# Order of the products of a half chunk: one PSUM bank after the other, or the two in turn

## The chip, the core and the metric

The kernel runs on one core of a Trainium2 chip. What counts is the device time of one execution in microseconds (us), the median of several runs.

## The reference, cut to what matters

Two transformer-like blocks and a mixture of experts on 256 tokens of 2048 features, all in float32: a layer with attention and a convolution, a layer with a spatial gate, a second block with attention and a state space branch, and last 16,384 experts as two dense products with sparse weights. Nearly all the work is in products of the activations with large weight matrices:

```
k, v, q, za, glu, zb = split(h @ ev_w_in)          # layer 0, 2048 x 5632
x = x + gate * (mix @ ev_w_out)                     # 2048 x 2048
p = h @ od_w_in ; x = x + gate * (mixed @ od_w_out) # layer 1, 2048 x 6144 and 2048 x 2048
... h @ w_in_2, w_attn_up_2, w_ssm_up_2, w_out_2    # second block
A = gelu(h @ peer_u.T) * weights ; x = x + gate * (A @ peer_v)   # experts, 2048 x 16384 twice
```

Between them stand norms with a scale and a shift, and each layer's scale, shift and gate come from a vector times a matrix of their own (the modulation).

## The kernel before, in words

**Chunks and halves.** Every large matrix is cut into chunks of 512 rows by 512 columns (1 MB), which come from memory in the order of one long plan. A chunk is worked off in two halves of 256 rows, that is two row tiles (`a` = 0, 1) of 128 rows. To keep float32 precision each half is split in two parts: ScalarE rounds it to `hi` (tile `whi`), VectorE makes `lo` = raw - `hi` (tile `wlo`). The activations are split the same way, `act.h` and `act.l` (tiles `hh` and `hl`, or `Ah`/`Al`, `mixh`/`mixl` and so on). A product is then three matmuls, hi with h, hi with l and lo with h, added up in PSUM.

**`gemm_part`** (L622) takes one half at a time and makes four tiles of 128 output features (`n` = 0 to 3) by 256 tokens. The weights are the stationary operand. The accumulator `ps` is 128 x 4 x 256 floats, that is two PSUM banks: `n` = 0 and 1 lie in the first, 2 and 3 in the second (or `ps` is a list of two tiles of one bank each, then named `last`). A half is 2 x 4 x 3 = 24 matmuls of 256 columns. There are 970 halves in all; 866 of them go through `gemm_part`.

**`gemm_tok_part`** (L646) makes keys, values, queries and the like, with tokens on the partitions: the activations are stationary, the weights stream through in 512 columns, and the two tiles of 128 tokens (`tt`) have a bank each (tiles `q`, `pv`, `kv`, `kvc`). A half is 2 x 2 x 3 = 12 matmuls of 512 columns. It serves the other 104 halves (52 chunks: group 4 to 6 of `ev`, 0 to 3 of `od`, 1 to 6 of `w2`, four chunks each); the first 8 of them do so for two activations, so there are 112 runs of 12 matmuls.

**The last half of an output projection** (`tiles` given, `j` = 1) has an order of its own, `n` outside and `a` inside, so that each pair of tiles can be read as soon as it is complete. There are four such halves.

**Who makes what, and when.** The program is written out in one thread of Python code; each engine runs its instructions in the order in which they were written. A clock (`Clock`, L256) estimates as the code runs when each engine will be done and when each tile will be there. After each half, `fill` (L552) asks `side` (L570) which other steps (evictions, norms, attention, the experts' weights) fit beside the products, by these estimates and in steps of 0.2 us; then the next halves are split, up to three ahead. A chunk of a modulation's matrix goes to VectorE as a multiply-add (tile `adaacc`), or, where the clock says that the products are more than `AGE` = 4 us past its arrival (`start`, L558), to TensorE (tile `adaps`). So the order in which side work stands on the engines depends on the estimated time of each product. The estimate lets a matmul start when its operands are there, and knows nothing of banks.

**The activations** of layer 1, the second block and the experts (`Normed`, L2105) are made in four groups of four row tiles by `h_group` (L851), each shortly before the first product needs it: VectorE `hu`, ScalarE `hh`, VectorE `hl`, row tile by row tile.

`forget` (L1528) makes eight forget gates: 48 matmuls of 256 columns in a row, with 8 columns of stationary weights, all into one place of one bank (tile `fp`).

Of the kernel before, what the change touches and what calls it, by code (L numbers as in the profile page):

```python
# [20 lines left out]
D = 2048  # L21
# [12 lines left out]
# ---------------------------------------------------------------- host layout  # L34
# [120 lines left out]
# ---------------------------------------------------------------- the plan of weight traffic  # L155
# [100 lines left out]
class Clock:  # L256
    """When each engine is expected to be through with what it has been given, and each part of a tile to be written and read."""
# [23 lines left out]
    def slot(self, tag, bufs, tile):  # L281
        """A new tile in one of the slots of a tag: written after the slot's last tile has been used."""
        slots = self.slots.setdefault(tag, [])
        if len(slots) == bufs:
            i = 0
            if tag in ("ms", "raw"):
                i = min(range(bufs), key=lambda i: self.used(slots[i]) if slots[i] in self.read else math.inf)
            self.parts[tile.tensor.name] = {(0, 1 << 20): [0.0, None, self.used(slots[i]), None]}
            del slots[i]
        slots.append(tile.tensor.name)  # L290
        return tile
# [4 lines left out]
    def free_at(self, tag, bufs, n):  # L296
        """When n of a tag's slots will have been read."""
        at = [0.0] * (bufs - len(self.slots.get(tag, [])))
        for name in self.slots.get(tag, []):
            if name in self.read:  # L300
                at.append(self.used(name))
        return sorted(at)[n - 1] if len(at) >= n else math.inf

    def columns(self, at, n):
        """The tensor engine's time for n columns: its clock is halved after a period in which it was mostly idle."""
# [39 lines left out]
class Timed:  # L345
    """The core's engines; each instruction is also entered in the clock."""
# [64 lines left out]
class Thread:  # L411
    """Work beside the weight stream. It yields the engine of its next step, with the number of PSUM slots that step takes
    (and when what it needs is there, if that isn't the last step's end); "w" when it waits for other threads."""
# [6 lines left out]
class K:  # L420
# [9 lines left out]
    # ---- storage  # L430
# [3 lines left out]
    def ms(self, name, shape=(128, 512), hold=False):  # L434
        """A PSUM bank, until something else than the tensor engine has read it, or, on hold, until its release."""
        t = self.psm.tile(list(shape), F32, name=name, tag="ms", bufs=4)
        return self.hold("ms", 4, t) if hold else self.clock.slot("ms", 4, t)
# [29 lines left out]
    # ---- weight stream  # L467
# [22 lines left out]
    def prep_hi(self, force):  # L490
        """The rounded part of the next half of a weight chunk."""
# [19 lines left out]
    def prep(self, force=True):  # L511
        """The rest of the next half chunk."""
# [11 lines left out]
    def ahead(self):  # L524
        """Keeps the split parts in front of the products: LOOK halves, and HILOOK more of their rounded parts."""
# [12 lines left out]
    # ---- side work  # L538
# [5 lines left out]
    def post(self, ps, gen, prio=0, eng="a"):  # L544
        """Work on products, once the tensor engine is through with what it has been given."""
# [6 lines left out]
    def fill(self, lead=LEAD):  # L552
        """After each half chunk of products: side work while these run, then the next parts of the weights."""
# [4 lines left out]
    def start(self, t):  # L558
        """When the next step of a thread could start."""
# [39 lines left out]
    def finish(self, *ts):  # L599
        """Runs these threads to their end, and others as far as they wait for them."""  # L600
# [14 lines left out]
    # ---- products  # L615
# [6 lines left out]
    def gemm_part(self, ps, name, g, kc, i, n_kc, act, kt0=0, tiles=None):  # L622
        """tiles: the work that follows on each of the four tiles of 128 features as soon as it is complete."""
        mm = self.nc.tensor.matmul
        for j in range(2):
            hi, lo = self.take(name, g, kc, j)
            each = tiles if j == 1 else None
            for n, a in [(n, a) for n in range(4) for a in range(2)] if each else [(n, a) for a in range(2) for n in range(4)]:
                kt = kt0 + 4 * i + 2 * j + a
                first, last = (kt == kt0), (kt == kt0 + 4 * n_kc - 1)  # L630
                s = slice(n * 128, n * 128 + 128)
                o = ps[n // 2][:, n % 2, :] if isinstance(ps, list) else ps[:, n, :]
                mm(o, hi[:, a, s], act.h(kt), start=first and n % 2 == 0, stop=False, skip_group_check=True)
                mm(o, hi[:, a, s], act.l(kt), start=False, stop=False, skip_group_check=True)
                mm(o, lo[:, a, s], act.h(kt), start=False, stop=last, skip_group_check=True)
                if each and a == 1 and n % 2 == 1:
                    each(n - 1)
                    each(n)
            if not each:
                self.fill(QUIET if tiles else LEAD)  # L640
# [5 lines left out]
    def gemm_tok_part(self, name, g, kc, i, n_kc, acts, outs):  # L646
        """outs[i]: two [128 tokens, 512] accumulators of activation i."""
        nc = self.nc
        for j in range(2):
            hi, lo = self.take(name, g, kc, j)  # L650
            for act, out in zip(acts, outs):
                if act is not acts[0]:
                    self.side(LEAD)
                for a in range(2):
                    kt = 4 * i + 2 * j + a
                    first, last = (kt == 0), (kt == 4 * n_kc - 1)
                    for tt in range(2):
                        s = slice(tt * 128, tt * 128 + 128)
                        nc.tensor.matmul(out[tt], act.h(kt)[:, s], hi[:, a, :], start=first, stop=False)
                        nc.tensor.matmul(out[tt], act.h(kt)[:, s], lo[:, a, :], start=False, stop=False)  # L660
                        nc.tensor.matmul(out[tt], act.l(kt)[:, s], hi[:, a, :], start=False, stop=last)
# [8 lines left out]
    # ---- modulation vectors  # L670
    def chunk(self, it, raw):
        """A chunk of a modulation's weights, worked off when it has come in: by the vector engine if that has the time."""
# [10 lines left out]
    def ada_s(self, it, raw):  # L683
        """Layer 0's shift and scale, 512 columns at a time, of x (row 0 of each 32) and of the context (row 16);
        each of the four row blocks of a chunk has its own 32 rows."""
# [32 lines left out]
    def ada(self, it, raw, me=None):  # L718
        """Its share of the vector: products on the tensor engine, or sums kept for each of the partitions."""
# [60 lines left out]
    # ---- norms  # L780
    def rsqrt_steps(self, out, ss, n, shape, v=None):
        """out = 1/sqrt(ss/n + EPS), or 1/sqrt(v) of a given v."""
# [15 lines left out]
    def stat(self, ps, r, first, last):  # L798
        """ps[t, half] += the sum of r over its partitions, for 256 tokens in two halves."""
# [3 lines left out]
    def spread(self, name, r):  # L803
        """A value per token, [128, 2], as a row on every partition."""
# [19 lines left out]
    def gap(self, until):  # L824
        """Modulation products while the tensor engine would wait."""
# [8 lines left out]
    def now(self, gen):  # L834
        """Runs a generator to its end and returns its value."""
# [6 lines left out]
    def sumsq(self, xg, g, ps, n=4):  # L842
        """Adds group g's squares into ps."""
# [7 lines left out]
    def h_group(self, act, g, xg, r, scale, shift, name):  # L851
        """One group of features of the split of (x r) scale + shift."""
# [25 lines left out]
    # ---- start  # L878
# [74 lines left out]
    def wait_mod(self, *keys):  # L953
        """Works off the plan and the threads until these vectors are there."""
# [8 lines left out]
    # ---- attention pieces  # L963
    def headnorm(self, ps, nh, gains, rope, dests, name):
        """ps: two [128 t, >= nh*128] views; per head rms over features, gain (and rope), then
        transposed into dests (one [128 hd, 256] view per head)."""
# [45 lines left out]
    def rope_tables(self):  # L1012
        """Gained rope tables of q and k: [128 t, 2, 128] each."""
# [14 lines left out]
    # ---- layer 0  # L1028
    def layer0(self):
# [30 lines left out]
        # the first groups, as the modulation of their inputs comes in  # L1060
# [12 lines left out]
        # keys and values  # L1073
# [73 lines left out]
    def gated(self, g, ps, gate):  # L1147
        """x += gate * ps for one group of features."""
# [6 lines left out]
    def out_proj(self, name, act, gate, kcs=range(4), nstat=1):  # L1155
        """x += gate * (act @ w), and the sums of squares of the new x."""
# [59 lines left out]
    def sum_ch(self, tiles, square):  # L1216
        """Sum over the channels of two [128, 4, 256] tiles: on every partition, or of the squares, a column per half."""
# [97 lines left out]
    # ---- layer 1  # L1315
# [102 lines left out]
    # ---- second block  # L1418
    def block2(self):
        nc = self.nc  # L1420
        # the norm of x2 = (x r1) fg: with r1 = rsqrt(ss0 / D + EPS), its rsqrt times r1 is rsqrt(ss1 / D + EPS (ss0 / D + EPS))
# [12 lines left out]
        # u, forget gates, q, k, v  # L1434
# [93 lines left out]
    def forget(self, h, bfc):  # L1528
        """Cumulated log forget gates, laid out for the two-row bias products."""
# [101 lines left out]
    # ---- state space branch  # L1631
    def exact_exp(self, x, n, tmp):
        """x <- exp(x) by range reduction and a polynomial; tmp: three [128, n] views."""
# [13 lines left out]
        # 2^k in two halves, so that each stays a normal number  # L1647
# [10 lines left out]
    def reduce_angle(self, x, k):  # L1658
        """x <- x - 2 pi round(x / 2 pi), within the sine's range."""
# [7 lines left out]
    def sincos(self, s, c, x):  # L1667
        """s, c <- sin x, cos x of a reduced angle."""
# [7 lines left out]
    def ssm_params(self):  # L1676
# [13 lines left out]
        # per state: decay and angle  # L1690
# [10 lines left out]
        # per channel and state: the input matrix  # L1701
# [127 lines left out]
    # ---- experts  # L1829
    def peer(self):  # L1830
# [43 lines left out]
        def before(g):  # L1874
            """x with what the earlier passes have come to."""
# [61 lines left out]
    def topk(self, g, q, ready, sk, sel, prev):  # L1937
# [20 lines left out]
        # sums of pairs (a, b) of the two sorted lists; with (a + 1)(b + 1) > 16 a pair is never among  # L1958
        # the first 16, so b < 8 is enough for a > 0: position 16 + 8 (a - 1) + b
# [44 lines left out]
    def top16(self, val, idx, s, w):  # L2004
        """The 16 largest of each row of s in order, with their places; w is for working on."""
# [19 lines left out]
    def expert_weights(self, tk, sel):  # L2025
        """The dense weights of all experts and tokens, by products of one-hots, into DRAM."""
# [49 lines left out]
    # ---- all  # L2076
# [28 lines left out]
class Normed(Split):  # L2105
    """(x r) scale + shift; a group of features is made shortly before a product first needs it."""
# [12 lines left out]
class LazySplit(Split):  # L2119
    """The experts' activations; a group is finished when a product first needs it."""  # L2120
# [28 lines left out]
```

## Time and profile before

| | |
|---|---|
| median of 3 runs | 3248.22 us |
| lowest and highest run | 3244.9 and 3250.54 us |
| span of the profiled execution, first to last instruction | 3244.0 us |
| TensorE busy | 3181.7 us (98%), 24,560 matmul records |
| VectorE busy | 2180.6 us (67%) |
| ScalarE busy | 1448.3 us (45%) |

The profiled execution has no time of its own beside its span; the span lies 4.2 us below the median of the runs, and what lies around it is taken to be that much. In the trace a matmul's start is recorded and its end is modelled (its duration covers the way through the array, so that neighbours overlap): the pace of a stream is read from starts, not from durations. A float32 matmul that isn't split shows as two records. All instructions have the line of one helper (L393), so they are told apart by tiles. The names show the operands as output<-inputs.

### The profile page before, as it was taken

How to read it: one execution, taken by the hardware profiler on the slowest of the kernel's cores; microseconds unless marked ns; L12 is line 12 of the kernel's file. 1: busy time of each engine (PE TensorE's matmuls, PEld its weight loads, DVE VectorE, ACT ScalarE, POOL GpSimd, SP SyncE). 2: the span in 40 equal slices, each digit the busy share in tenths (PEclk: the TensorE clock that was granted, in tenths of full speed). 3: DMA queues.
4: the chain of work that ended last, by engine and by line, in shares of the span. 5: the costliest groups of instructions: out<-in, count | busy, mean ns of one | idle time of the engine just before them, and what ended most of it. 6: DMA issues, size and time to landing. Idle time of an engine off the chain costs nothing.

```text
span 3244.0 us, 58103 instructions
## 1 busy us (share of the span) xinstructions
PE 3181.7 (98%) x24560; PEld 2954.1 (91%) x24560; DVE 2180.6 (67%) x3266; ACT 1448.3 (45%) x1879; POOL 12.2 (0%) x24
## 2 busy tenths in 40 slices
PE   5999999999999999999999999999999999999999
PEld 3677789789997778999999999999999999999999
DVE  3488868877788877667789996555455445445544
ACT  2334544444445556444444554444344334434433
POOL 0000000000000000000000000000000000000000
PEclk8999999999999999999999999999999999999999
DMA  7878586788785655677755667665555555555653
GB/s 305 319 285 299 195 312 236 279 319 306 279 305 208 222 195 193 253 258 293 288 180 199 236 228 273 234 208 202 182 202 207 185 190 205 198 184 203 228 195 130
DMA packets 140484, 764.04 MB, mean 236 GB/s; under 512 B 12528, under 2 KB 45296, under 8 KB 53568
## 3 DMA queue, kind: packets, MB, share of 16 engines
q1 hardware_dynamic: 137248, 750.04, 64.1%
q0 software_dynamic: 1824, 6.37, 0.6%
q8 instruction: 192, 3.15, 0.4%
q10 hardware_dynamic: 1152, 3.93, 0.3%
q14 instruction: 68, 0.56, 0.0%
HBM read 739.32 MB, written 20.97 MB: 234 GB/s over the span
## 4 chain that ended last, share of the span: by engine, by line
PE 93%; DVE 3%; DMA 2%; ACT 1%; issue 0%; DVEq 0%; SPq 0%; ACTq 0%; POOLq 0%
PE ps L393 73%; PE q L393 5%; PE last L393 3%; PE adaps L393 3%; PE pv L393 2%; PE pw L393 2%; DMA raw<-in_ev_dram 1%; DVE wlo L393 1%; PE S L393 1%; PE kvc L393 1%; PE kv L393 1%; DMA raw<-in_evo_dram 1%; PE po L393 0%; PE bu L393 0%; DVE cacc L393 0%; PE py L393 0%
## 5 line engine op out<-in xcount | busy, mean ns | idle before, releaser
L393 DVE TENSOR_TENSOR wlo<-raw,whi 128x1024 fp32r<-128x1024 f32 x970 | 1181.9, 1222 | 847.9 <-PE ps L393 619.8
L393 ACT ACTIVATE whi<-raw 128x1024 fp32r<-128x1024 f32 x970 | 1023.0, 1059 | 1384.4 <-PE ps L393 1032.2
L393 PE MATMUL ps<-hh,whi 128*128 128x256 f32 x3904 | 1120.0, 287 | 16.2 <-ACT hh L393 12.1
L393 PE MATMUL ps<-hl,whi 128*128 128x256 f32 x3904 | 1109.2, 284 | 1.2
L393 PE MATMUL ps<-hh,wlo 128*128 128x256 f32 x3904 | 1108.0, 284 | 0.0
L393 PEld LDWEIGHTS ps<-hh,whi 128*128 128x128 f32 x3904 | 752.1, 193 | 56.9 <-issue 33.6
L393 PEld LDWEIGHTS ps<-hl,whi 128*128 128x128 f32 x3904 | 752.6, 193 | 3.9 <-DVE hl L393 3.6
L393 PEld LDWEIGHTS ps<-hh,wlo 128*128 128x128 f32 x3904 | 752.3, 193 | 0.0
L393 PE MATMUL ps<-Ah,whi 128*128 128x256 f32 x1920 | 543.5, 283 | 0.0
L393 PE MATMUL ps<-Al,whi 128*128 128x256 f32 x1920 | 543.4, 283 | 0.0
L393 PE MATMUL ps<-Ah,wlo 128*128 128x256 f32 x1920 | 543.4, 283 | 0.0
L393 PEld LDWEIGHTS ps<-Ah,whi 128*128 128x128 f32 x1920 | 368.6, 192 | 0.8 <-issue 0.8
L393 PEld LDWEIGHTS ps<-Al,whi 128*128 128x128 f32 x1920 | 368.6, 192 | 0.0
L393 PEld LDWEIGHTS ps<-Ah,wlo 128*128 128x128 f32 x1920 | 368.6, 192 | 0.0
L393 DVE SCALAR_TENSOR_TENSOR adaacc<-raw,silc,adaacc 128x1024 f32<-128x1024 f32 x126 | 158.2, 1279 | 9.4 <-DMA raw<-in_ada_dram 9.0
L393 PE MATMUL ps<-mixh,whi 128*128 128x256 f32 x416 | 119.0, 286 | 0.0
L393 PE MATMUL ps<-mixh,wlo 128*128 128x256 f32 x416 | 117.7, 283 | 0.7 <-DVE wlo L393 0.7
L393 PE MATMUL ps<-mixl,whi 128*128 128x256 f32 x416 | 117.6, 283 | 0.0
L393 PE MATMUL q<-whi,hh 128*128 128x512 f32 x256 | 102.9, 402 | 0.0
L393 PE MATMUL q<-whi,hl 128*128 128x512 f32 x256 | 99.9, 390 | 0.0
L393 PE MATMUL q<-wlo,hh 128*128 128x512 f32 x256 | 99.9, 390 | 0.0
L393 DVE SCALAR_TENSOR_TENSOR cacc<-ypad,pk,cacc 128x256 f32<-128x256 f32 x240 | 99.3, 479 | 0.0
(389 smaller groups left out, 3618.4 us busy)
## 6 DMA issues: line engine op xcount, KB each, us to landing
raw<-in_ada_dram SPq DMA_DIRECT2D x160, 1024.0 KB, 5.4
raw<-in_pu_dram SPq DMA_DIRECT2D x128, 1024.0 KB, 4.8
raw<-in_pv_dram SPq DMA_DIRECT2D x128, 1024.0 KB, 4.8
raw<-in_w_dram SPq DMA_DIRECT2D x60, 1024.0 KB, 4.8
raw<-in_od_dram SPq DMA_DIRECT2D x48, 1024.0 KB, 5.9
raw<-in_ev_dram SPq DMA_DIRECT2D x44, 1024.0 KB, 6.5
raw<-in_ada0s_dram SPq DMA_DIRECT2D x32, 1024.0 KB, 7.8
raw<-in_evo_dram SPq DMA_DIRECT2D x16, 1024.0 KB, 5.9
```

Source lines behind the costliest of these rows:

```text
L393: r = f(*args, **kw)
```

## The change

The three matmuls of a product no longer follow each other. In `gemm_part`, for each row tile `a`, the four tiles of features all take hi with h, then all take hi with l, then all take lo with h, and the tiles come in the order 0, 2, 1, 3, so that each matmul writes another bank than the one before it; before it were six in a row to one bank and then six to the other. The last half of an output projection keeps its order. In `gemm_tok_part` the two tiles of tokens, a bank each, come in turn; before it were three in a row to each. The numbers of matmuls, weight loads, bytes and every other instruction's own work are the same; the `start` flag still stands on the first matmul into a bank and on no other.

```diff
-            for n, a in [(n, a) for n in range(4) for a in range(2)] if each else [(n, a) for a in range(2) for n in range(4)]:
+            first, last = kt0, kt0 + 4 * n_kc - 1
+
+            def product(n, a, p):
                 kt = kt0 + 4 * i + 2 * j + a
-                first, last = (kt == kt0), (kt == kt0 + 4 * n_kc - 1)
-                s = slice(n * 128, n * 128 + 128)
                 o = ps[n // 2][:, n % 2, :] if isinstance(ps, list) else ps[:, n, :]
-                mm(o, hi[:, a, s], act.h(kt), start=first and n % 2 == 0, stop=False, skip_group_check=True)
-                mm(o, hi[:, a, s], act.l(kt), start=False, stop=False, skip_group_check=True)
-                mm(o, lo[:, a, s], act.h(kt), start=False, stop=last, skip_group_check=True)
-                if each and a == 1 and n % 2 == 1:
-                    each(n - 1)
-                    each(n)
-            if not each:
-                self.fill(QUIET if tiles else LEAD)
+                w = (hi, hi, lo)[p][:, a, n * 128:n * 128 + 128]
+                mm(o, w, act.l(kt) if p == 1 else act.h(kt), start=kt == first and n % 2 == 0 and p == 0, stop=kt == last and p == 2,
+                   skip_group_check=True)
+
+            if each:
+                for n in range(4):
+                    for a in range(2):
+                        for p in range(3):
+                            product(n, a, p)
+                    if n % 2 == 1:
+                        each(n - 1)
+                        each(n)
+                continue
+
+            for a in range(2):
+                for p in range(3):
+                    for n in (0, 2, 1, 3):
+                        product(n, a, p)
+            self.fill(QUIET if tiles else LEAD)
...
-                    for tt in range(2):
-                        s = slice(tt * 128, tt * 128 + 128)
-                        nc.tensor.matmul(out[tt], act.h(kt)[:, s], hi[:, a, :], start=first, stop=False)
-                        nc.tensor.matmul(out[tt], act.h(kt)[:, s], lo[:, a, :], start=False, stop=False)
-                        nc.tensor.matmul(out[tt], act.l(kt)[:, s], hi[:, a, :], start=False, stop=last)
+                    for p in range(3):
+                        for tt in range(2):
+                            s = slice(tt * 128, tt * 128 + 128)
+                            nc.tensor.matmul(out[tt], (act.l if p == 2 else act.h)(kt)[:, s], (lo if p == 1 else hi)[:, a, :],
+                                             start=first and p == 0, stop=last and p == 2)
```

The rest of the diff takes out comments.

## Rows read from the trace of the kernel before

**Rows 1.** The page: span, engines' busy time, and the chain that ended last.
```profile
span 3244.0 us, 58103 instructions
PE 3181.7 (98%) x24560; PEld 2954.1 (91%) x24560; DVE 2180.6 (67%) x3266; ACT 1448.3 (45%) x1879; POOL 12.2 (0%) x24
...
PE 93%; DVE 3%; DMA 2%; ACT 1%; issue 0%; DVEq 0%; SPq 0%; ACTq 0%; POOLq 0%
```

**Rows 2.** The chain in order of time: start, length, tile, number of instructions.
```profile
627.90 49.19 PE pv L393 x216
...
1016.20 5.47 PE fp L393 x48
...
2105.11 1088.63 PE ps L393 x9072
```

**Rows 3.** A stretch by engine: busy time, with PEclk and DMA share behind.
```profile
2105.00:3193.00 1088.00, 1088.00 (x9069) 1088.00 (x9069) 549.72 (x471) 445.11 (x426) 0.00 (x0) 1.00 0.57 198
```

**Rows 4.** Timeline of TensorE where one `gemm` ends and another begins (2502.38).
```profile
2502.26 0.28 PE L393 MATMUL ps<-hh,wlo 128*128 128x256 f32 x1
2502.38 0.28 PE L393 MATMUL ps<-Ah,whi 128*128 128x256 f32 x1
...
2502.98 0.28 PE L393 MATMUL ps<-Ah,wlo 128*128 128x256 f32 x1
2503.10 0.28 PE L393 MATMUL ps<-Ah,whi 128*128 128x256 f32 x1
```

**Rows 5.** Timeline of TensorE, products with tokens on the partitions.
```profile
640.43 0.39 PE L393 MATMUL pv<-wlo,hh 128*128 128x512 f32 x1
640.66 0.39 PE L393 MATMUL pv<-whi,hl 128*128 128x512 f32 x1
640.89 0.39 PE L393 MATMUL pv<-whi,hh 128*128 128x512 f32 x1
```

**Rows 6.** Waits of TensorE and its weight loads: total us, times, longest.
```profile
PE ps L393 <- ACT hh L393: 12.1, 8, 2.3
...
PE ps L393 <- DVE wlo L393: 0.7, 1, 0.7
...
PEld ps L393 <- DVE hl L393: 3.6, 12, 0.3
```

**Rows 7.** Timeline at the second group of the experts' activations.
```profile
1603.12 0.48 DVE L393 SCALAR_TENSOR_TENSOR hl<-hu,mod,hh 128x256 fp32r<-128x256 f32 x1 [0.18 <-ACT hh L393]
1603.14 0.39 PE L393 MATMUL ps<-hh,whi 128*128 128x256 f32 x1
...
1603.66 0.39 PE L393 MATMUL ps<-hl,whi 128*128 128x256 f32 x1
1603.88 0.28 PE L393 MATMUL ps<-hh,wlo 128*128 128x256 f32 x1
```

**Rows 8.** Timeline at the start of layer 0's output projection.
```profile
499.43 0.39 PE L393 MATMUL ps<-mixh,whi 128*128 128x256 f32 x1
499.65 0.28 PE L393 MATMUL ps<-mixl,whi 128*128 128x256 f32 x1
500.60 0.38 PE L393 MATMUL ps<-mixh,wlo 128*128 128x256 f32 x1 [0.68 <-DVE wlo L393]
...
501.41 0.28 PE L393 MATMUL ps<-mixh,wlo 128*128 128x256 f32 x1
```

**Rows 9.** The chain where a modulation chunk stands among products on TensorE.
```profile
1847.16 0.99 PE adaps L393 x8
1848.16 3.07 PE ps L393 x24
...
1857.68 2.87 PE ps L393 x24
```

**Rows 10.** Groups by line and tile: count, busy time, mean ns, idle before.
```profile
L393 DVE SCALAR_TENSOR_TENSOR adaacc<-raw,silc,adaacc 128x1024 f32<-128x1024 f32 x126 | 158.2, 1279 | 9.4 <-DMA raw<-in_ada_dram 9.0
...
L393 PE MATMUL adaps<-raw,silc 128*32 128x512 f32 x704 | 95.4, 612 | 0.0
```

## The prediction

> **What bounds the kernel now.** Read the page first [rows 1]: TensorE is busy for 3181.7 of 3244.0 us, and the chain that ended last is 93% TensorE. So the time is the number of matmuls times their pace, plus some 62 us of idle time (3244.0 - 3181.7), most of it where a stage starts. The chain in order of time shows the pace [rows 2]: in the experts' stage 9072 matmuls follow each other without a pause in 1088.63 us, 0.1200 us for each. The table by stretch [rows 3] says of the same stretch that TensorE is busy for all of it, VectorE for half (549.72 of 1088), DMA for 0.57, and that the clock is granted in full (1.00, the 2.4 GHz level). Nothing else is late there. Two things can change the time: the pace, and the waits outside such stretches.
>
> **The pace, matmuls of 256 columns.** 866 halves of 24 are 20,784 matmuls; less the four halves that keep their order (96) the change moves 20,688. It takes none away. One thousandth of a microsecond at each is 20.7 us, so the question is what a neighbour in the same bank costs. The kernel before answers this itself, since it does both: every sixth matmul goes to another bank. In the timeline the `gemm` that begins at 2502.38 has its first six products in the first bank, 2502.38 to 2502.98, five steps in 0.60 us; the seventh, at 2503.10, is the first in the other bank, and comes 0.12 us later [rows 4]. The step from 2502.26 to 2502.38, into another accumulator altogether, takes 0.12 us as well. If staying in a bank were what made the pace 0.120, the steps out of it would be shorter, and they are not.
>
> A second sign: `forget` writes 48 matmuls of the same 256 columns in a row into one place of one bank, and does it in 5.47 us, 0.114 us each [rows 2]. Staying in a bank forever goes faster than the mixed stream; what differs is that its weights have 8 columns. So I take nothing for the pace. Bounds: the timeline is read to 0.01 us, and five steps in 0.60 us fix the step within a bank to 0.002; a saving at a switch smaller than 0.01 us would not show in one row. As the lower end I take the nearest row that is faster, 0.114: (0.120 - 0.114) x 20,688 = 124 us. As the upper end, a switch that costs something: at 1,512 switches among 9072 matmuls the mean is 0.1200 and each step read is 0.12, so again less than 0.01 us, and I take a tenth of that, 0.001 us, on the 5 of 6 that become switches: 0.001 x 20,688 x 5/6 = 17 us. I choose zero, since both kinds of step stand side by side with one length.
>
> **The pace, 512 columns.** 112 runs of 12 are 1,344 matmuls. 216 of them take 49.19 us, 0.228 each, the few stops included [rows 2]. Three in a row go to one bank: 640.43 to 640.66 stays in it, 640.66 to 640.89 leaves it, 0.23 us each [rows 5]. Nothing again; 0.006 us at each, as above, would be 8 us.
>
> The Trainium skill bears on this from two sides. "Perfetto Trace Analysis", Matmul Optimizations, advises that all 8 PSUM banks be used for the most instruction-level parallelism, which speaks for the change; these rows show no such gain at a switch. "TensorE: Matmul & The Clock Gate", Part 2, says of the drain step that the engine's connection to PSUM is one write-only port, and that one matmul's drain overlaps the next one's fill anyway; by that another bank gives nothing, and the rows agree. Part 1 there gives N / 2.4 plus about 2.5 ns between starts, 109 ns for 256 columns against the 120 of the row; were the bank the reason for the difference, an estimate from that page would be 11 ns x 20,688, some 228 us.
>
> **Operands that are needed later.** This is what the new order does change. hi with l was the 2nd matmul of a row tile and becomes the 5th; lo with h was the 3rd and becomes the 9th. Where the wait for `l` or `lo` ends last, three to six matmuls of 0.12 us now run in it. The table of waits says how often that is [rows 6]: weight loads wait for `hl` 12 times, 3.6 us in all, for `wlo` once, 0.7 us. An example of the first [rows 7]: the first product of a group starts at 1603.14, `hl` ends at 1603.12 + 0.48 = 1603.60, the second product comes at 1603.66. In the new order three more with `hh` fill that hole of 0.52 us, and 0.52 - 0.12 = 0.40 us is won. Twelve times would be 4.8 us. But a group's gain is lost if the next group's `hh` comes late (`PE ps <- ACT hh`, 8 times, 12.1 us [rows 6]), because TensorE then only waits longer; VectorE and ScalarE, which set that moment, start no earlier. I keep one gain per stage, for layer 0, layer 1, the second block and the experts: 4 x 0.40 = 1.6 us. For `wlo` [rows 8]: now products 1, 2 run and the third waits until 500.60; the ninth starts at 501.41. In the new order the ninth is the one that starts at 500.60, 0.81 us earlier. The next half's `wlo` comes of the same late transfers, so I keep 0.6. Both ends: nothing is kept, 0; all is kept, 4.8 + 0.8 = 5.6 us. Sum: 2.2 us.
>
> Two small moves cost nothing. `whi` is read for the last time by the 20th matmul of a half and no longer by the 23rd, which frees its buffer 0.36 us earlier; TensorE is the bound, not the splitting, so nobody gains. The accumulator's second bank is first written by the 2nd matmul and no longer by the 7th, 0.6 us earlier; with two accumulators its last reader had at least one `gemm` of 48 matmuls (5.8 us) for it, and that hides it; without that cover a `gemm` would wait up to 0.6 us.
>
> **The written order of the side work.** The clock in the code lets a product start when its operands are there, so its estimates move by a few tenths of a microsecond wherever `l` or `lo` was expected late, from the first stage on; side work is placed in steps of 0.2 us, so some steps will stand elsewhere. What this can cost is seen at the modulation chunks. One on TensorE takes 0.99 us, and the 24 products behind it 3.07 instead of 2.87 [rows 9]: 1.2 us of the chain. One on VectorE takes 2 x 1.279 us beside the products. 704 records at 8 a chunk are 88 chunks on TensorE; 126 multiply-adds at 2 a chunk are 63 on VectorE, besides the first of a vector [rows 10]. A chunk that changes sides is worth 1.2 us either way. I expect a few, in both directions: 0, with 8 chunks, 9.6 us, as the bound on each side.
>
> **Sum.** The profiled execution of 3244.0 us becomes 3244.0 - 2.2 = 3241.8; with the 4.2 us by which the median lies above the span, 3246.0 us.
>
> **The rivals.**
> *The pace falls.* If a neighbour in the same bank does hold back a matmul in a way that a single switch in six hides, the pace could come to that of the fastest row, 0.114: 3246 - 124 - 8 = 3114 us. For it: 0.120 is more than `forget` needs, so something beyond the columns limits these matmuls. Against it: the steps at a switch [rows 4, 5], and that `forget` is faster without any switch. Chance 0.05.
> *The side work falls better.* Six modulation chunks fewer on TensorE, with the 2.2 us, make 3246 - 6 x 1.2 = 3239 us. For it: an earlier estimate for the products makes fewer chunks count as late, so the drift is rather to VectorE, which is idle for a third. Against it: the estimate moves by tenths, the limit is 4 us. Chance 0.11.
> *Slower: the side work falls worse.* Ten more chunks on TensorE, 12 us: 3258 us. It decides from (6.5 + 2.2) / 1.2, some 8 chunks. For it: TensorE has no room, every chunk there lengthens the chain; against it: the direction above. A switch that costs 0.001 us would do the same, 3246 + 17 = 3263 us, and counts here; the rows show none. Chance 0.10.
> That the change does not do what it says is no rival: in the order 0, 2, 1, 3 each neighbour lies in the other bank, also from one of the three rounds to the next.
>
> **How the numbers follow.** The forecast (pace unchanged, 2 us won, few chunks moved) has 0.74, the rivals 0.05, 0.11 and 0.10. A measurement of this kernel can tell about 0.2%, 6.5 us, from no change: 3241.7 to 3254.7. The forecast's own cases lie within it, the first two rivals are faster, the third slower: 0.16, 0.74, 0.10. The range takes the bound of the side work on both sides, 3246 +/- 9.6: 3236 to 3256; beyond it lie the fallen pace and part of the last two cases, some 0.15.
>
> **What would show it.** In the experts' stretch the 9072 matmuls should again take 1088.6 us, 0.120 each, with the tiles' names in runs of four (`Ah,whi` four times, `Al,whi` four times, `Ah,wlo` four times). The waits for `hl` and `wlo` should shrink, and those for `hh` grow a little. The number of `adaps` records should stay near 704. The prediction is wrong if a step in that stretch is anything but 0.120 us, by 20.7 us for each thousandth, or if `adaps` records change by more than 64.

## The result and the profile after

The change makes the kernel slower: 3308.28 us (median of 4 runs, 3302.54 to 3317.41) against 3249.38 us for the kernel before on the same chip (4 runs), a ratio of 1.0181 with the interval 1.0167 to 1.0195, some 59 us. The prediction was 3246 us and no difference. One of the 12 runs of the kernel with the new order under the old plan, below, took 4391.18 us at a granted clock of 0.653, and the ratios leave it out.

The page of the kernel after, beside [rows 1]: the span, the busy time of the engines, and the shares of the chain that ended last.

```profile
span 3300.7 us, 58231 instructions
...
PE 3198.7 (97%) x24640; PEld 2956.2 (90%) x24640; DVE 2156.9 (65%) x3248; ACT 1443.0 (44%) x1880; POOL 12.2 (0%) x24
...
PE 90%; DVE 4%; DMA 4%; ACT 1%; issue 1%; DVEq 0%; ACTq 0%; POOLq 0%
PE ps L393 69%; PE q L393 5%; PE adaps L393 4%; PE last L393 3%; PE pv L393 2%; DMA raw<-in_od_dram 2%; PE pw L393 2%; DVE wlo L393 1%; DMA raw<-in_ev_dram 1%; PE kvc L393 1%; DVE cacc L393 1%; PE kv L393 1%; PE S L393 1%; ACT whi L393 1%; PE bu L393 0%
```

TensorE is busy for 17.0 us more, and it idles for 39.7 us more (3300.7 - 3198.7 = 102.0 against 62.3). In the chain DMA has gone from 2% to 4%, and the weights of layer 1 (`in_od`) alone hold 2%. So this does not look like the pace of a stream; something waits for memory. The chain and the timeline of TensorE in the experts' stage say so too:

```profile
2161.75 1088.64 PE ps L393 x9072
```
```profile
2559.02 0.64 PE L393 MATMUL ps<-Ah,whi 128*128 128x256 f32 x4
2559.50 0.64 PE L393 MATMUL ps<-Al,whi 128*128 128x256 f32 x4
2559.98 0.64 PE L393 MATMUL ps<-Ah,wlo 128*128 128x256 f32 x4
```

The runs of four are there, each starts 0.48 us after the one before it, and the 9072 products take 1088.64 us against 1088.63 [rows 2]. The bank of the neighbour is worth nothing here. With 512 columns it is the same: in the kernel after pairs of `pv` matmuls start at 587.57 and 588.03, 0.23 us for each as in [rows 5].

**Where the time went.** The table by stage places it: first of the kernel before, then of the kernel after. The stages are layer 0 from 235 us to its end, layer 1, the second block, and the experts. The columns are the stretch, its length, the busy time of TensorE, weight loads, VectorE, ScalarE and GpSimd, the granted clock, the DMA share and GB/s.

```profile
235.00:575.91 340.91, 337.59 (x2453) 279.99 (x2445) 267.91 (x516) 159.14 (x217) 7.02 (x11) 1.00 0.73 263
575.91:981.25 405.34, 400.86 (x2948) 367.07 (x2948) 319.61 (x362) 192.31 (x225) 1.07 (x2) 0.99 0.80 295
981.25:1596.60 615.35, 610.30 (x4282) 535.99 (x4282) 471.27 (x620) 309.49 (x415) 1.07 (x2) 1.00 0.65 237
1596.60:3244.00 1647.40, 1642.81 (x13706) 1633.92 (x13706) 988.14 (x1501) 708.31 (x907) 0.00 (x0) 1.00 0.58 205
```
```profile
235.00:583.85 348.85, 340.15 (x2453) 281.42 (x2445) 262.39 (x490) 159.89 (x218) 7.02 (x11) 0.99 0.71 259
583.85:1041.44 457.59, 420.51 (x3021) 370.30 (x3021) 304.44 (x372) 190.45 (x226) 1.07 (x2) 0.97 0.70 259
1041.44:1653.60 612.16, 606.85 (x4282) 535.17 (x4282) 471.15 (x620) 307.27 (x414) 1.07 (x2) 1.00 0.65 238
1653.60:3300.00 1646.40, 1642.37 (x13706) 1633.96 (x13706) 988.10 (x1501) 706.40 (x907) 0.00 (x0) 1.00 0.58 205
```

Layer 0 ends 7.9 us later (583.85 against 575.91), and layer 1 takes 52.3 us longer (457.59 against 405.34). The second block and the experts win 3.5 us (615.35 - 612.16, and 1647.4 against 3300.7 - 1653.6 = 1647.1), which makes the 56.7 us between the two spans. Of these four stages layer 1 had the most DMA traffic (a share of 0.80), and now its weights come more slowly: 259 instead of 295 GB/s. Its matmul records grew by 73; over the whole kernel `adaps` has 776 records of modulation chunks against 704 [rows 10], nine chunks more.

**The first loss.** ScalarE at the end of layer 0, in the timeline, before and after; the bracket is the idle time ahead of a row and what ended it.

```profile
571.74 0.81 ACT L393 ACTIVATE sq<-x 128x256 f32<-128x256 f32 x2 [4.26 <-DVE x L393]
573.18 0.81 ACT L393 ACTIVATE sq<-x 128x256 f32<-128x256 f32 x2 [0.63 <-DVE x L393]
...
580.75 1.99 ACT L393 ACTIVATE whi<-raw 128x1024 fp32r<-128x1024 f32 x2
```
```profile
564.12 1.06 ACT L393 ACTIVATE whi<-raw 128x1024 fp32r<-128x1024 f32 x1 [0.88 <-PE last L393]
577.00 1.06 ACT L393 ACTIVATE whi<-raw 128x1024 fp32r<-128x1024 f32 x1 [11.80 <-DMA raw<-in_od_dram]
577.96 1.32 ACT L393 ACTIVATE sq<-x 128x256 f32<-128x256 f32 x4
```

Before, the last four squares (`sq`) of layer 0, from which layer 1's norm is made, run as soon as `x` is there. After, a rounding of weights (`whi`) stands ahead of them in ScalarE's queue, and its 256 rows have not come in yet: ScalarE is idle for 11.80 us until its transfer has landed, and the squares behind it wait as well. TensorE goes idle, and layer 1's norm is 7.9 us late. The kernel after had been 1.9 us ahead until then (its last `x` starts at 570.73 in VectorE's timeline, against 572.66), so the end of layer 0 lost 9.9 us: some 7.2 until the squares are done, and the rest behind TensorE's pause of 7.72 us, where the granted clock is 0.50 (578.41 to 583.85) and not 1.00.

**The second loss.** In layer 1 itself the table of waits has three rows that were small or not there. Before, ScalarE's rounding waited for layer 1's weights 5 times, 10.4 us in all.

```profile
ACT whi L393 <- DMA raw<-in_od_dram: 157.8, 40, 11.8
...
PE adaps L393 <- DVE adaacc L393: 22.3, 1, 22.3
...
PEld ps L393 <- ACT whi L393: 22.6, 25, 2.3
```

The chain shows what such a wait looks like, and that it comes again and again (DMA of `in_od` holds 31.7% of the chain between 780 and 830 us):

```profile
788.01 1.04 PE adaps L393 x8
...
789.07 4.95 DMA raw<-in_od_dram
...
794.12 1.07 ACT whi L393
...
798.74 6.03 DMA raw<-in_od_dram
```

A modulation chunk is worked off on TensorE, that frees its buffer, the next transfer starts only then and takes 5 us, and ScalarE and VectorE split what came. At the layer's end stands the 22.3 us wait of TensorE for a gate that is not complete, while the output projection stands behind it:

```profile
924.69 1.21 DVE adaacc L393
...
925.92 4.99 DMA raw<-in_ada_dram
...
930.93 3.69 DVE adaacc L393 x3
...
934.66 3.00 PE adaps L393 x8
...
938.99 34.55 PE ps L393 x288
```

**The theory.** Raw weight chunks come into four buffers (`RAW`). The plan holds back the first three chunks of layer 1's gate: they stay in their buffers until `gap` lets them go, as a filler for TensorE's pause at the layer's start.

```python
for t in [t for t in self.threads if t.flex]:
    if max(t.wake, c.t["pe"]) < until - 0.5:
        t.held = False
        ...
        self.step(t)
```

With the products in another order, the code's clock expects other moments, and one `whi` is written ahead of the squares. That moves the estimates at the pause, where they also price TensorE at half clock after idling; the test then lets one chunk fewer go, and the third stays in one of the four buffers until the gate is asked for at the layer's end. Why the test turns over is read from the code. That one chunk fewer goes is seen in TensorE's timeline of the pause: three chunks of eight products in the kernel before, two in the kernel after.

```profile
574.63 1.06 PE L393 MATMUL adaps<-raw,silc 128*32 128x512 f32 x8
577.05 3.05 PE L393 MATMUL adaps<-raw,silc 128*32 128x512 f32 x16
```
```profile
581.92 1.93 PE L393 MATMUL adaps<-raw,silc 128*32 128x512 f32 x8
584.93 1.46 PE L393 MATMUL adaps<-raw,silc 128*32 128x512 f32 x8
```

So the theory (call it **domino**) has two prices: the queue at the end of layer 0, and a weight stream on three buffers in layer 1. Rivals: **banks**, that the new order itself is slow on TensorE outside of the experts' stage; **records**, that the nine more chunks on TensorE are the cost, as the prediction would have priced them (9 x 1.2 = 11 us).

### The profile page after: what moved, and what is told of

Same layout as the page of the kernel before. It is cut to its first block, busy times and chain, and to the rows that moved or that the text cites. A ratio compares the mean times of both kernels' runs of the same rounds, so it can differ in the third digit from the quotient of the medians.

```text
span 3300.7 us, 58231 instructions
## 1 busy us (share of the span) xinstructions
PE 3198.7 (97%) x24640; PEld 2956.2 (90%) x24640; DVE 2156.9 (65%) x3248; ACT 1443.0 (44%) x1880; POOL 12.2 (0%) x24
## 4 chain that ended last, share of the span: by engine, by line
PE 90%; DVE 4%; DMA 4%; ACT 1%; issue 1%; DVEq 0%; ACTq 0%; POOLq 0%
PE ps L393 69%; PE q L393 5%; PE adaps L393 4%; PE last L393 3%; PE pv L393 2%; DMA raw<-in_od_dram 2%; PE pw L393 2%; DVE wlo L393 1%; DMA raw<-in_ev_dram 1%; PE kvc L393 1%; DVE cacc L393 1%; PE kv L393 1%; PE S L393 1%; ACT whi L393 1%; PE bu L393 0%
## 5 line engine op out<-in xcount | busy, mean ns | idle before, releaser
L393 PE MATMUL ps<-hh,whi 128*128 128x256 f32 x3904 | 642.8, 287 | 24.1 <-ACT hh L393 14.2
L393 PE MATMUL ps<-hh,wlo 128*128 128x256 f32 x3904 | 630.6, 284 | 0.4
L393 PE MATMUL ps<-hl,whi 128*128 128x256 f32 x3904 | 629.5, 284 | 0.0
L393 PEld LDWEIGHTS ps<-hh,whi 128*128 128x128 f32 x3904 | 539.3, 192 | 70.3 <-issue 25.3
L393 PEld LDWEIGHTS ps<-hh,wlo 128*128 128x128 f32 x3904 | 540.6, 193 | 2.6 <-DVE wlo L393 2.6
L393 PEld LDWEIGHTS ps<-hl,whi 128*128 128x128 f32 x3904 | 540.4, 192 | 0.0
L393 PE MATMUL ps<-Ah,whi 128*128 128x256 f32 x1920 | 308.8, 283 | 0.0
L393 PE MATMUL ps<-Al,whi 128*128 128x256 f32 x1920 | 308.6, 283 | 0.0
L393 PE MATMUL ps<-Ah,wlo 128*128 128x256 f32 x1920 | 308.6, 283 | 0.0
L393 PE MATMUL adaps<-raw,silc 128*32 128x512 f32 x776 | 107.1, 611 | 0.0
```

Of the source, the lines that this page charges most:

```text
L393: r = f(*args, **kw)
```

## The experiments

**Order alone, plan alone.** Both kernels issue one order to TensorE and tell the clock the other. The first runs the new order, with all side work where it stood before; the second runs the old order with the side work of the kernel after.

```diff
-                for p in range(3):
-                    for n in (0, 2, 1, 3):
-                        product(n, a, p)
+                for n, p in [(n, p) for p in range(3) for n in (0, 2, 1, 3)]:
+                    product(n, a, p, self.chip)
+                for n, p in [(n, p) for n in range(4) for p in range(3)]:
+                    product(n, a, p, self.planned)
```

This is the first kernel, against the kernel after, cut to `gemm_part`: `chip` goes to TensorE only, `planned` to the clock only. In the second kernel the two lists change places, and `gemm_tok_part` is treated alike in both.

> The products run in the new order, but the clock is told of them in the old order, so that every other instruction stands where it stood in the kernel before. Placement theory (the order itself is neutral on the chip, the loss is where the side work was written): the time of the kernel before, 3249 us, less the 0 to 5.6 us of operands needed later, so 3244 to 3250; 9072 products again in 1088.6 us. Order theory (the alternation itself, or what it frees or needs later, costs on the chip): most of the 59 us, 3290 to 3310.

Measured: 3242.24 us (median of 12 runs) against 3249.25, ratio 0.9981 (0.9972 to 0.9990), a little below the expected 3244. All of ScalarE's 1879 instructions stand in the order of the kernel before. Its experts' products, in the chain:

```profile
2097.83 1088.63 PE ps L680 x9072
```

> The reverse: products in the old order, the clock told of the new one, so that all other instructions stand as in the changed kernel. Placement theory: 3300 to 3315 us, layer 1 some 458 us long (405 in the kernel before). Order theory: about 3249 us.

Measured: 3313.95 us, ratio 1.0196 (1.0180 to 1.0213), with 776 records of `adaps` as in the kernel after, and with its waits (156.0 us of rounding for `in_od`, 22.5 us for the gate). So the whole loss is the plan's and none of it comes from the order on TensorE: **banks** falls. The order itself is a gain of some 6 us, more than the prediction's 2.2.

**The kernel after, with the held chunks let go.** After the pause whatever is still held is released and treated like any other chunk.

```diff
         if gap:
             self.gap(self.clock.t["act"] + 1.3)
+            for t in self.threads:
+                t.held = False
```

> The changed kernel with one rule more: modulation chunks that are held back at the start of a layer are let go once the gap they were held for is past. One-chunk theory (a chunk of layer 1's gate stays in one of the four raw buffers through the whole layer, and the weight stream runs on three): layer 1 falls from 458 to some 405 us, the time from 3308 to 3250 to 3260 us, with some 8 us left from the end of layer 0. Many-steps theory (nine more chunks on TensorE and other moved steps each cost a little): less than a third comes back, over 3285 us. Order theory: over 3290 us.

Measured: 3256.16 us, ratio 1.0018 (1.0009 to 1.0027). Layer 1 is back to its old length and its old DMA share, while the rounding ahead of the squares is still there (window of layer 1; ScalarE's timeline):

```profile
585.23:991.40 406.17, 400.69 (x2945) 366.68 (x2944) 323.45 (x385) 191.54 (x222) 1.07 (x2) 0.99 0.80 291
```
```profile
578.38 1.06 ACT L393 ACTIVATE whi<-raw 128x1024 fp32r<-128x1024 f32 x1 [9.54 <-DMA raw<-in_od_dram]
579.35 1.32 ACT L393 ACTIVATE sq<-x 128x256 f32<-128x256 f32 x4
```

One buffer is what layer 1 lost. 52.1 us came back (3308.28 - 3256.16), though only eight modulation chunks left TensorE (712 records), which at 1.2 us each are 9.6: **records** falls as well. The chunks on TensorE rather follow from the buffer: in the kernel below, where nothing but the buffer is taken from the kernel before, six more chunks go there (752 records).

**The kernel before, with one chunk kept.** The reverse: nothing is changed but that the third held chunk is not let go in the pause.

```diff
         for t in [t for t in self.threads if t.flex]:
+            if t.mod[:2] == (1, 2) and sum(u.flex and u.held for u in self.threads) == 1:
+                continue
             if max(t.wake, c.t["pe"]) < until - 0.5:
```

> The kernel before, products in the old order, with one modulation chunk (the third of layer 1's gate) kept in its raw buffer until the gate is asked for. One-chunk theory: layer 1 lengthens by 40 to 65 us, 3290 to 3315 us in all, with a hole on TensorE of about 20 us before the output projection of layer 1. Many-steps theory and order theory: under 3265 us.

Measured: 3286.32 us, ratio 1.0107 (1.0090 to 1.0124). The loss is 37 us, somewhat less than expected; why it is 15 us less than what the release gave back was not traced. Its marks in the profile are those of the kernel after (window of layer 1; waits):

```profile
573.31:1021.90 448.59, 416.03 (x2996) 370.25 (x2992) 301.85 (x348) 189.57 (x223) 1.07 (x2) 0.97 0.72 266
```
```profile
ACT whi L393 <- DMA raw<-in_od_dram: 127.6, 34, 8.3
...
PE adaps L393 <- DVE adaacc L393: 17.5, 1, 17.5
```

**The kernel after, without the early rounding.** In the fill behind the second last half of an output projection (`QUIET`, the stretch ahead of the squares) only weights are rounded that the clock expects to be there by then, instead of up to `ARRIVE` = 6 us later. Nothing is released by hand.

```diff
-        if not force and self.clock.used(raw.tensor.name) > self.clock.t["pe"] + ARRIVE:
+        if not force and self.clock.used(raw.tensor.name) > self.clock.t["pe"] + self.arrive:
...
+        self.arrive = 0.0 if lead == QUIET else ARRIVE
         self.ahead()
+        self.arrive = ARRIVE
```

> The changed kernel, products in the new order, with one rule: before the last half of an output projection no further weight is rounded that isn't expected to be there already. Up to layer 1 this moves one ScalarE instruction, the rounding of layer 1's first chunk, from before the last four squares of layer 0 to behind them; no chunk is let go by hand. Domino theory (that instruction waits for its transfer with the squares behind it, TensorE's pause lengthens, the clock in the code therefore prices its products at half speed, and the third held chunk no longer fits the gap and stays): both the 8 us at the end of layer 0 and the 52 us of layer 1 come back, 3243 to 3255 us. If the two losses are independent: only the 8 us, some 3300 us.

Measured: 3248.63 us, ratio 1.0002 (0.9992 to 1.0011). Both losses are gone at once, with 704 records of `adaps`. ScalarE has the squares on time again, and layer 1 has its length:

```profile
569.38 0.81 ACT L393 ACTIVATE sq<-x 128x256 f32<-128x256 f32 x2 [4.62 <-DVE x L393]
570.82 0.81 ACT L393 ACTIVATE sq<-x 128x256 f32<-128x256 f32 x2 [0.63 <-DVE x L393]
...
578.40 1.99 ACT L393 ACTIVATE whi<-raw 128x1024 fp32r<-128x1024 f32 x2
```
```profile
573.60:979.00 405.40, 400.61 (x2936) 366.41 (x2936) 324.99 (x387) 193.65 (x224) 1.07 (x2) 0.99 0.80 294
```

Up to the pause ScalarE's order differs from that of the kernel after in this rounding alone, and the pause again holds three chunks (8 products at 572.27, 16 at 574.69). This is the domino's link in the plan of the kernel after: where the rounding does not stand ahead of the squares, the third chunk fits into the pause and the buffer is free, although nobody asked for that.

**How near the edge the plan stood.** Two small changes of a constant that the product order has nothing to do with: in the kernel before, `AGE` from 4 to 3 (shown); in the kernel after, `AGE` from 4 to 3.5.

```diff
-AGE = 4.0
+AGE = 3.0
```

> The kernel before, products in the old order, with one constant of the clock changed: a modulation chunk counts as late after 3 us, not 4. If the plan of the kernel before stands on an edge, an unrelated change of this kind also leaves the third held chunk in its buffer: 3280 to 3310 us, layer 1 over 440 us. If the edge is a matter of the product order alone: 3245 to 3260 us.

> The changed kernel with the same constant at 3.5 us. Edge theory: no chunk is left, layer 1 some 405 us, 3245 to 3262 us. If the new order makes the loss by itself: 3295 to 3315 us.

Measured: the kernel before with `AGE` 3 takes 3288.94 us (2 runs), ratio 1.0125 (1.0107 to 1.0144), and in its layer 1 rounding waits 128.7 us for `in_od` (38 times), the gate 17.4 us. The kernel after with 3.5 takes 3254.97 us, ratio 1.0018 (1.0008 to 1.0029), and there the wait for `in_od` is 13.7 us. So one constant puts the same loss into the old order and takes it out of the new one.

In neither of these two does a rounding that waits for its transfer stand ahead of the squares (they start at 572.62 and 571.82, as soon as `x` is there), and in both TensorE's pause ends when VectorE has added up squares (`sqr`), and the first chunk behind it takes 1.93 us; yet one lets two chunks go and the other three. So the rounding is one way into the loss and not the only one, and half clock in the pause does not decide it; which estimate turns the test over is not shown. The count of chunks in the pause does go with the loss: two in the kernel after, in its plan with the old order, with one chunk kept and with `AGE` 3, which all pay for it in layer 1; three in the kernel before, under the old plan, without early rounding, with `AGE` 3.5 and in the version below, which don't. With the release there are two, and the third follows at 591.53.

**A version to beat both.** The kernel after with the release shown above and another bound for rounding early.

```diff
-ARRIVE = 6.0
+ARRIVE = 5.0
```

> The changed kernel with held chunks let go after the gap and with weights rounded at most 5 us (not 6) ahead of their expected arrival: an attempt at a version of the new order that needs no separate book-keeping. Placement theory: both losses gone, 3238 to 3250 us, layer 1 some 403 us. Order theory has fallen already.

Measured: 3247.32 us, ratio 0.9999 (0.9990 to 1.0008): level with the kernel before. The new order under the old plan, at 3242.24, stays the best version that was run; it beats both kernels.

**What the 6 us are.** Two kernels under the old plan take the parts of the new order apart. One keeps the late operands and goes in runs of two and four to one bank (in its order 0, 1, 2, 3 and then 3, 2, 1, 0 a row tile has runs of 2, 4, 4 and 2, and not of four only, as its expectation below says); the other writes another bank at each step and needs `l` and `lo` as early as before. Shown are their lists for `gemm_part`, the first kernel's and then the second's; `gemm_tok_part` has lists of the same kind.

```diff
+                for n, p in [(n, p) for p in range(3) for n in ((3, 2, 1, 0) if p == 1 else (0, 1, 2, 3))]:
...
+                for n, p in [(0, 0), (2, 1), (0, 2), (2, 0), (0, 1), (2, 2), (1, 0), (3, 1), (1, 2), (3, 0), (1, 1), (3, 2)]:
```

> The clock still sees the order of before, so the side work on ScalarE, VectorE and the queues stands as before. On TensorE the three rounds of the new order are kept (hi with l is the 5th to 8th matmul of a row tile, lo with h the 9th to 12th), but the tiles go 0, 1, 2, 3 in the first and third round and 3, 2, 1, 0 in the second, so that neighbours come in runs of four to one bank (before it was runs of six, and in the change runs of one). Theory that the 6 to 8 us which the new order won under the old plan come from operands needed later: 3241 to 3244 us, as there. Rival, that they come from the change of banks: 3247 to 3251 us, as before.

Measured: 3243.63 us, ratio 0.9985 (0.9976 to 0.9994).

> The clock still sees the order of before. On TensorE neighbours always write different banks, but the operands are needed as early as before: tile 0 hi with h, tile 2 hi with l, tile 0 lo with h, and so on, so that l is needed by the 2nd matmul of a row tile and lo by the 3rd. Theory that the gain under the old plan comes from operands needed later: 3246 to 3251 us, no gain. Rival, that it comes from the change of banks: 3241 to 3244 us. Both theories expect the 9072 matmuls of the experts to take 1088.6 us again.

Measured: 3249.98 us, ratio 1.0008 (0.9999 to 1.0017). The wait of weight loads for `hl` is there again, as in [rows 6], and it is in neither of the two kernels with late operands; the experts' products are what they were:

```profile
PEld ps L682 <- DVE hl L393: 3.3, 11, 0.3
```
```profile
2109.54 1088.63 PE ps L682 x9072
```

So the gain comes from operands that are needed later, and the change of banks, made alone, wins nothing. The two intervals of the kernels with late operands overlap, and neither reaches the one of the kernel without. The granted clock does not explain it: its mean is 0.9926 in the kernel with late operands in runs of two and four, and 0.9924 in the kernel before beside it. In which stage the 6 us are won stays open: a single profile moves by as much (this kernel's span is 3248.5 us, that of the one before it 3246.5, with medians 6 us apart).

## Why the prediction was wrong, point by point

**The pace, 256 and 512 columns.** Right. 0.1200 us for each of the 9072 matmuls in every kernel that was run, whatever the order. The bound of 124 us that was drawn from `forget`'s 0.114 was far from anything that happened.

The Trainium skill's "TensorE: Matmul & The Clock Gate", Part 2, describes the connection to PSUM as one write-only port and says that the drain of one matmul overlaps the fill of the next; the prediction drew from it that another bank gives nothing. The kernel that only changes the banks agrees with that, at 1.0008.

**Operands that are needed later.** Right in kind, too small in size. The text put 2.2 us on it and 5.6 us as the end; alone, under the old plan, it gave 0.19%, some 6 us (interval 0.10% to 0.28%, 3 to 9 us). The waits moved as the text said: under the old plan those of `ps`'s weight loads for `hl` (3.6 us) and `wlo` (0.9 us) are gone, and TensorE's for `hh` grow from 12.1 to 14.3 us. (The 0.7 us for `wlo` in [rows 6] is TensorE's own row, which the text took for the weight loads'.) These waits alone are not 6 us, so it is not shown that "I keep one gain per stage" was the place where the term came out too small.

**The written order of the side work.** This is the step that failed: "A chunk that changes sides is worth 1.2 us either way. I expect a few, in both directions: 0, with 8 chunks, 9.6 us, as the bound on each side." Nine more chunks did go to TensorE, which the text had named as the mark of a wrong prediction, and the sign was that of the slower rival. That mark came true for another reason than the one given for it: eight of the nine go back to VectorE when the buffer is released. The price was taken from TensorE's time alone [rows 9], and that is not where a misplaced step costs. The runs put two other prices in its place:
- a step that waits in an engine's queue holds up all that stands behind it. One rounding ahead of four squares, 11.80 us idle, and TensorE's start of layer 1 is 7.9 us late. With the loss of layer 1 taken out by the release, 1.0018 against the 0.9981 of the same order under the old plan is left, some 12 us; that difference holds the rounding and whatever else that plan moves.
- a chunk that is worked off late keeps its buffer. One of four buffers held through layer 1 costs 37 us in the kernel before and 52 us in the kernel after, in a stage whose DMA share was 0.80. Both could be seen before: the share by stage was in the windows, and `RAW` and the held chunks in the code. The text read the windows for the experts' stage alone [rows 3], which at 0.57 has room.

The direction argued there ("the drift is rather to VectorE") was not borne out either: with the kept chunk out of the way the new order has 712 records of `adaps` (release) or 704 (no early rounding). As the code reads, the estimates moved only a little, but one threshold turned over, and what followed was much larger than the move; the estimates themselves are in no trace.

**Sum.** -6 us from the order, and some +64 from its plan (the ratio of the plan alone, 1.0196), give +58 us, against 59 measured. The plan's part is those two prices, which the release and the early rounding each take out, and which are not quite separate; the 6 to 7 us that remain between the kernel without early rounding (1.0002) and the new order under the old plan (0.9981) were not traced to a step.

**What stays open.** The first place where the order written by the two plans differs lies far ahead of the rounding, in layer 0 (ScalarE's `adasb` at 111.13 us in the kernel after, 120.14 in the kernel before); which of the small moves in between tips it was not tried. Nor was the plan searched for settings: five plans with the new order ran from 0.9999 to 1.0181 of the kernel before, so the plan decides more than the order.

## What to carry to other kernels

Where a program schedules itself by an estimated clock, an edit that changes an estimate is two edits, and each can be measured alone: give the engine one order and the clock the other. Price a moved step by what it holds (its place in an in-order queue, its buffer), and not by its own duration; look for the stage where DMA has the least room and ask what one buffer fewer would do there. What a neighbour in another bank is worth was read from two kinds of step that already stood side by side in the trace, and that reading held.

## What the hardware showed that was not expected

A held buffer is dear: with three of four 1 MB buffers layer 1's traffic falls from 295 to 259 GB/s and the stage grows by 13%, the wait at its end included, although on the average of the stage the DMA engines are then idle for 30% of the time. And a pause of TensorE costs more than its length. In the first window below, the end of the 22.3 us wait for the gate, TensorE does nothing for 9.9 us and the granted clock is 0.50, the 1.2 GHz level; in the next it is still 0.69, and over the rest of the stage 1.00. What half clock costs is read at layer 1's start: behind the pause of 7.72 us, at 0.50, the eight products of a modulation chunk take 1.93 us (581.92 in the timeline above), and 1.06 in the kernel before at 1.00 (574.63). The eight products that add up the gate's sums took 3.00 us behind the long wait, against 1.00 in the running stream of the kernel before (`adaps` at 503.49 in its chain, last row), but that is not the clock alone: the second four start at 935.85, when VectorE's last sum is done (930.93 + 4.87 = 935.80 in its timeline).

```profile
924.69:934.60 9.91, 0.00 (x0) 0.00 (x0) 4.87 (x6) 0.00 (x0) 0.00 (x0) 0.50 0.38 116
934.60:938.99 4.39, 3.63 (x14) 1.04 (x15) 1.20 (x2) 1.31 (x2) 0.00 (x0) 0.69 0.88 358
939.00:1041.44 102.44, 101.67 (x849) 98.13 (x848) 78.54 (x82) 43.77 (x57) 1.07 (x2) 1.00 0.75 268
```
```profile
503.49 1.00 PE adaps L393 x8
```
